# Scan products in four quadrants and a hand-laid engine order in the attention loop of a hybrid attention and delta-net layer

## Chip, cores and metric

One NeuronCore of one Trainium2 chip. The metric is the device time of one execution in microseconds; the measured time is the median of several executions. TensorE has a granted clock with two levels, 1.2 and 2.4 GHz; the profile gives it as a share of the higher one.

## The reference, cut to what matters

One layer over 2048 latent tokens on a grid 64 wide, with 256 context tokens as a prefix, in fp32. Two branches read one input projection: neighbourhood attention (8 heads of 64, a window of 8 x 16 keys plus all context keys in one softmax) and a gated DeltaNet that runs a recurrence over chunks of 64 tokens, forward and backward.

```python
def step(S, xs):                                   # one chunk of the delta rule
    qk_i, qd_i, kd_i, u_i, w_i, gt_i = xs
    v_new = u_i - einsum('bhck,bhkv->bhcv', w_i, S)
    o_i = einsum('bhck,bhkv->bhcv', qd_i, S) + einsum('bhij,bhjv->bhiv', qk_i, v_new)
    S = S * gt_i[..., None, None] + einsum('bhck,bhcv->bhkv', kd_i, v_new)
    return S, o_i
...
s = concat([s_win, s_ctx]); pr = softmax(s)        # attention, per head and query row
o = einsum(p_win, v_band) + einsum(p_ctx, vc)
...
o_dn = _rmsnorm(o_f + rev(o_b)) ; y = sigmoid(g_na)*u_na + sigmoid(g_dn)*u_dn ; x + gate * (y @ w_out)
```

## The kernel before

The program runs in stages: projections of the normed tokens (TensorE), triangular solves on VectorE beside them, neighbourhood keys and bias tables, then a loop over 32 attention units with the recurrence inside it, then the output projections. The change lies in the loop.

An attention unit is 128 queries (8 rows of 16 columns) of four heads, taken as two pairs `pr`. For a pair, `scores` multiplies queries and banded keys as three products of high and low parts into two PSUM tiles `pw`, and VectorE adds the bias table (`tedge` at the grid's rim, `tmid` elsewhere) and takes the maximum (L1078). `scores_ctx` does the same with the context keys (maxima L1085, merged in L1087) and ScalarE takes the four exponentials (L1090, L1093). `turn` transposes the banded weights (L1101, copies L1103), `turn_ctx` those of the context (L1110, copy L1112), `values` multiplies both with the values (L1121, L1125). `sums_inv` inverts the sums and GpSimd spreads them into `rb`; `finish` transposes `rb` and multiplies the output with it and with the gate path (L1141, L1142). The banded keys come in four widths: 288, 360, 384 and 512.

The recurrence is a Python generator, `scan`, of which `pump(chain, n)` runs n pieces between the steps of a unit, so that one step of the recurrence, forward and backward chunk side by side on the two halves of the partitions, falls into each unit. Each piece of products is 16 products of 64x64x64, 8 heads by 2 directions, which the profile shows as 32 matmuls: both state products (L871), the third `p2` (L887, copied to `cw` by ScalarE, L889), `p4` for the state (L894, added in L895) and `p3` for the output (L901, L903). A direction d multiplies on row half d and column half d of the array. GpSimd multiplies the state by its decay (L883) and, in the last 16 units, adds the output of the opposite direction (L881). There `dn_out` also normalises the output of the step before: square (L917), row sums (L919, L920), a power on GpSimd (L922), scaling (L923), transposes (L927), product with the gate path (L928) and a store.

What sets the order: within the loop TensorE runs in the order of the program text (`tc.manual_schedule`). VectorE, ScalarE, GpSimd and SyncE, which issues every DMA, run in the order that the planner lays from its costs and priorities; only the splits of new queries and keys into a high part (ScalarE, L966) and a low part (GpSimd, L967), the weight splits (L1197, L1200) and the gate products (L1165) are kept in program order among themselves. Queries are loaded for two units at a time in even units and split in the odd unit that follows; new key rows are split in units 1 to 5, 9, 10, 13, 14 and 17 to 19. PSUM has 3 tiles `pw`, 2 `pt`, 2 `pc` and 1 `po`; `cr` and `cw` have one buffer, the loaded operands of a step two.

## Time and profile before

| | |
|---|---|
| median of 3 runs | 2399.5 us (2392.4 to 2406.4) |
| the profiled execution | 2395.0 us |
| its span, first to last instruction | 2393.3 us |
| mean granted clock of TensorE | 0.971 |
| busy: TensorE, VectorE, ScalarE, GpSimd | 2197.7, 1501.5, 850.4, 938.6 us |
| the unit loop | about 1478 to 2016 us of the span |

Times below are microseconds from the first instruction of the profiled execution. PE is TensorE's matmuls and PEld its weight loads, DVE is VectorE, ACT ScalarE, POOL GpSimd, SP SyncE. A matmul's end is modelled by the profiler, its start is measured, so distances are taken from start to start. A bracket behind an instruction is the time that its engine stood idle before it and what released it.

### The profile page before, as it was taken

How to read it: one execution, taken by the hardware profiler on the slowest of the kernel's cores; microseconds unless marked ns; L12 is line 12 of the kernel's file. 1: busy time of each engine (PE TensorE's matmuls, PEld its weight loads, DVE VectorE, ACT ScalarE, POOL GpSimd, SP SyncE). 2: the span in 40 equal slices, each digit the busy share in tenths (PEclk: the TensorE clock that was granted, in tenths of full speed). 3: DMA queues.
4: the chain of work that ended last, by engine and by line, in shares of the span. 5: the costliest groups of instructions: out<-in, count | busy, mean ns of one | idle time of the engine just before them, and what ended most of it. 6: DMA issues, size and time to landing. Idle time of an engine off the chain costs nothing. (4 is left out here: it accounts for less than half of the span.)

```text
span 2393.3 us, 47334 instructions
## 1 busy us (share of the span) xinstructions
PE 2197.7 (92%) x18359; PEld 1842.7 (77%) x18359; DVE 1501.5 (63%) x2410; ACT 850.4 (36%) x2624; POOL 938.6 (39%) x784
## 2 busy tenths in 40 slices
PE   6999999998989999999889987899888887999999
PEld 2778777876767778999878866777767776889988
DVE  3736777469959969859759803666566766222222
ACT  4524344344333332434554112444444444211110
POOL 2514777654423102315757410211123335543442
PEclk8999999999999999999999998999999999999999
DMA  7323444665574152154676567777886776444342
GB/s 266 102 75 77 114 123 125 159 154 140 145 189 123 54 128 89 58 133 133 179 185 185 166 166 216 218 195 198 215 209 188 188 199 189 142 118 129 108 115 90
DMA packets 461593, 358.17 MB, mean 150 GB/s; under 512 B 203254, under 2 KB 386698, under 8 KB 460810
## 3 DMA queue, kind: packets, MB, share of 16 engines
q1 hardware_dynamic: 461368, 355.16, 55.3%
q8 instruction: 144, 2.36, 0.4%
q14 instruction: 81, 0.66, 0.1%
HBM read 231.71 MB, written 119.67 MB: 147 GB/s over the span
## 5 line engine op out<-in xcount | busy, mean ns | idle before, releaser
L179 PE MATMUL pd<-hT,slots 128*128 128x512 f32 (+1 forms) x3360 | 813.5, 397 | 1.8 <-ACT hT L319 1.7
L179 PEld LDWEIGHTS pd<-hT,slots 128*128 128x128 f32 x3360 | 619.9, 191 | 147.2 <-issue 3.8
L580 DVE TENSOR_TENSOR tmp<-Xs 128x236 f32<-128x236 f32 (+43 forms) x310 | 315.5, 1018 | 38.7 <-DMA Xs<-d_X 25.9
L582 DVE TENSOR_TENSOR Xs<-Xs,tmp 128x236 f32<-128x236 f32 (+43 forms) x310 | 321.1, 1036 | 8.6
L125 POOL TENSOR_TENSOR slots<-w_raw,slots 128x512 fp32r<-128x512 f32 (+1 forms) x76 | 115.7, 1523 | 348.6 <-ACT slots L124 339.4
L729 PE MATMUL pd<-slots,hT 128*128 128x256 f32 x1248 | 164.0, 292 | 0.0
L729 PE MATMUL pd<-wide,hT 128*128 128x256 f32 x1248 | 159.5, 290 | 2.4 <-ACT wide L124 1.3
L729 PEld LDWEIGHTS pd<-slots,hT 128*128 128x128 f32 x1248 | 158.9, 196 | 0.0
L729 PEld LDWEIGHTS pd<-wide,hT 128*128 128x128 f32 x1248 | 156.4, 196 | 3.2 <-ACT wide L124 1.7
L1090 ACT ACTIVATE pr<-pr,nm 128x288 f32<-128x288 f32 (+3 forms) x128 | 77.9, 609 | 161.4 <-DVE nm L1087 161.4
L883 POOL TENSOR_TENSOR sd<-sd,gts 128x512 f32<-128x512 f32 x36 | 37.6, 1045 | 215.9 <-PE pc L871 198.3
L1346 DVE SCALAR_TENSOR_TENSOR gt<-gt,pu 128x256 f32<-128x256 f32 x120 | 46.3, 418 | 121.0 <-DMA gt<-d_g 73.6
L782 POOL TENSOR_TENSOR tmk<-trr,tmk 128x288 f32<-128x288 f32 (+3 forms) x72 | 98.0, 1378 | 40.1 <-DMA tmk<-in_k_mk_dram 35.5
L484 DVE SCALAR_TENSOR_TENSOR y<-raw,vT,y 128x512 f32<-128x512 f32 (+1 forms) x112 | 95.5, 864 | 24.8 <-ACT raw L472 21.2
L1345 PE MATMUL pu<-ckq,OS 128*128 128x256 f32 x512 | 95.2, 284 | 2.2 <-DVE gt L1346 1.3
L1360 DVE SCALAR_TENSOR_TENSOR ckd<-pf,gate 128x512 f32<-128x512 f32 x32 | 22.0, 692 | 119.7 <-PE pf L1356 111.8
L694 POOL TENSOR_TENSOR nrn<-nss,nhalf 128x8 f32<-128x8 f32 x34 | 72.6, 2135 | 54.7 <-DVE nss L693 54.4
L1347 POOL TENSOR_TENSOR gt<-gt 128x256 f32<-128x256 f32 x60 | 44.3, 738 | 122.3 <-DVE gt L1346 110.3
L205 ACT ACTIVATE zt<-pd 128x512 f32<-128x512 f32 x68 | 40.4, 594 | 142.8 <-PE pd L179 68.8
L1348 ACT CAST yh<-gt 128x256 fp32r<-128x256 f32 x60 | 24.3, 405 | 187.6 <-POOL gt L1347 187.2
L873 DVE TENSOR_TENSOR cr<-pc,egs 128x512 f32<-128x512 f32 x68 | 46.8, 688 | 66.2 <-DMA cT<-d_T 36.0
L1101 PE MATMUL pt<-ident,pr 128*128 128x128 f32 (+2 forms) x416 | 66.3, 286 | 23.5 <-ACT pr L1090 22.4
(295 smaller groups left out, 4612.7 us busy)
## 6 DMA issues: line engine op xcount, KB each, us to landing
w_raw<-in_w_in_dram SPq DMA_DIRECT2D x92, 256.0 KB
ckq<-d_kq SPq DMA_DIRECT2D x64, 256.0 KB
gt<-d_g SPq DMA_DIRECT2D x60, 256.0 KB
d_X<-X SPq DMA_DIRECT2D x72, 128.0 KB
Xs<-d_X SPq DMA_DIRECT2D x18, 512.0 KB
d_g<-zt SPq DMA_DIRECT2D x36, 256.0 KB
cv<-d_v SPq DMA_DIRECT2D x72, 128.0 KB
cT<-d_T SPq DMA_DIRECT2D x72, 128.0 KB
```

The source lines that it names most:

```text
L125: G.tensor_tensor(out=lo[:, j:j + 4, 0:n], in0=wr, in1=hi[:, j:j + 4, 0:n].bitcast(F32), op=ALU.subtract)
L179: PE.matmul(ps[0:n, 0:m], a[:, k, 0:n], h_part(g, z, k), start=k == 0 and i == 0, stop=k == KB - 1 and i == 2)
L484: V.scalar_tensor_tensor(out=y[:, 0:m], in0=raw[:, o + j - 1:o + j - 1 + m], scalar=tap(j), in1=y[:, 0:m], op0=ALU.mult, op1=ALU.add)
L580: V.tensor_tensor(out=tv, in0=X[r, piv, cols].unsqueeze(1).to_broadcast([8 * n, m, w]), in1=X[r, rows, piv].unsqueeze(2).to_broadcast([8 * ...
L582: V.tensor_tensor(out=X[r, rows, cols], in0=X[r, rows, cols], in1=tv, op=ALU.add)
L694: G.tensor_tensor(out=rn, in0=ss, in1=nhalf, op=ALU.pow)
L729: PE.matmul(ps[:, 256 * i:256 * i + 256], h[:, 256 * j + P * i:256 * j + P * i + P], w[:, :, part, k, :], start=k == 0 and n == 0, stop=k ...
L782: G.tensor_tensor(out=mv, in0=rr[:, k0:k0 + nr, w0:w0 + n], in1=mv, op=ALU.add)
L873: V.tensor_tensor(out=t, in0=ps, in1=eg, op=ALU.mult)
L1090: S.activation(e[:, 0:nk], e[:, 0:nk], AF.Exp, bias=nm[:, u:u + 1], accum_out=self.sums[:, hh, 0:1])
L1101: PE.transpose(ptw[0:kb, b, :], self.et[u][:, kb * b:kb * b + kb], ident)
L1345: PE.matmul(ps, a, r[:, k, :], start=k == 0 and n == 0, stop=k == 3 and n == 2)
```

## The change

Four things are changed.

- In a main step of the recurrence the two state products are issued as one group, head by head, the second one with its output on the opposite column half (`half[d ^ z]`), into a second PSUM tile; `p4` and `p3` likewise become one group, `p3` on the opposite half. The output of the two directions therefore lies with its halves swapped, and `dn_tokens` swaps the two halves of its addresses; `egw` holds the growth factors with the halves swapped. The steps over the context tokens keep their groups.
- In the unit, `scores` of the second pair stands between `turn` and `turn_ctx` of the first, `scores` of the next unit between `turn` and `turn_ctx` of the second pair, `values(1)` behind the next unit's `scores_ctx`, and `sums_inv` behind the second `turn`. There are five pumps in a unit instead of seven: the state products ahead of the first turn; `cr` of the second product and the square of `dn_out` behind `scores(1)`; decay, `p2`, `cw`, and row sums, power and scaling of `dn_out` behind `scores_ctx(1)`; the transposes of `dn_out` behind `values(0)`; `p4` and `p3` behind the next `scores(0)`.
- VectorE, ScalarE and GpSimd run in the order of the program text through the loop, as TensorE does. SyncE stays with the planner.
- `turn_ctx` always copies on ScalarE (before: VectorE for the first pair); `rb` has one buffer instead of two; `tedge` is allocated in the pool `ap`, which opens once the projections' pools are closed, instead of `aq`, which opens earlier.

```diff
@@ -187,8 +187,8 @@
         v = d.rearrange("q (n s t) -> q n s t", s=2, t=C)
         c0, n = t0 // C, m // C
         if c0 >= 16:
-            return v[:, c0 - 16:c0 - 16 + n, 0]
-        return v[:, 16 - c0 - n:16 - c0, 1][:, ::-1]
+            return v[:, c0 - 16:c0 - 16 + n, 1]
+        return v[:, 16 - c0 - n:16 - c0, 0][:, ::-1]
 
 
     def gate_col(kind, i, p):
@@ -861,22 +861,24 @@
             main = i >= CCH
             ld = scan_in.pop(i)
             scan_load(i + 1)
-            eg = egs[:, i].unsqueeze(2).to_broadcast([P, H, C])
             half = [slice(C * d, C * d + C) for d in range(2)]
 
-            def times_state(z):
-                ps = pc.tile([P, H, C], F32, name="pc")
-                for h in range(H):
+
+            pss = [pc.tile([P, H, C], F32, name="pc") for _ in range(2 if main else 1)]
+            for h in range(H):
+                for z, ps in enumerate(pss):
                     for d in range(2):
-                        PE.matmul(ps[half[d], h, :], ld["ckq"][half[d], ho(h), z, :], sd[half[d], h, :], start=True, stop=True)
+                        PE.matmul(ps[half[d ^ z], h, :], ld["ckq"][half[d], ho(h), z, :], sd[half[d], h, :], start=True, stop=True)
+
+            def grown(z, e):
                 t = q2.tile([P, H, C], F32, name="cr")
-                V.tensor_tensor(out=t, in0=ps, in1=eg, op=ALU.mult)
+                V.tensor_tensor(out=t, in0=pss[z], in1=e.unsqueeze(2).to_broadcast([P, H, C]), op=ALU.mult)
                 return t
             r = ld["cv"]
-            V.tensor_tensor(out=r, in0=r, in1=times_state(0), op=ALU.subtract)
+            V.tensor_tensor(out=r, in0=r, in1=grown(0, egs[:, i]), op=ALU.subtract)
             yield
             if main:
-                tq = times_state(1)
+                tq = grown(1, egw[:, i - CCH])
                 if i - CCH >= 16:
                     G.tensor_tensor(out=tq.rearrange("p h e -> p (h e)"), in0=tq.rearrange("p h e -> p (h e)"), in1=os_[:, NCH - 1 - i], op=ALU.add)
                 yield
@@ -888,17 +890,18 @@
             w = q2.tile([P, H, C], F32, name="cw")
             S.copy(w, p2)
             yield
+
             p4 = pc.tile([P, H, C], F32, name="pc")
+            p3 = pc.tile([P, H, C], F32, name="pc") if main else None
             for h in range(H):
                 for d in range(2):
                     PE.matmul(p4[half[d], h, :], ld["ckd"][half[d], h, :], w[half[d], h, :], start=True, stop=True)
+                for d in range(2 if main else 0):
+                    PE.matmul(p3[half[1 - d], h, :], ld["cA"][half[d], ho(h), :], w[half[d], h, :], start=True, stop=True)
             V.tensor_tensor(out=sd, in0=sd, in1=p4, op=ALU.add)
-            yield
+            if not main:
+                yield
             if main:
-                p3 = pc.tile([P, H, C], F32, name="pc")
-                for h in range(H):
-                    for d in range(2):
-                        PE.matmul(p3[half[d], h, :], ld["cA"][half[d], ho(h), :], w[half[d], h, :], start=True, stop=True)
                 o = q2.tile([P, H, C], F32, name="co", bufs=2)
                 V.tensor_tensor(out=o, in0=tq, in1=p3, op=ALU.subtract)
                 if i - CCH < 16:
@@ -915,6 +918,7 @@
         def dn_out(t, oa, zd):
             ob = q2.tile([P, H, C], F32, name="ob", bufs=2)
             S.activation(ob, oa, AF.Square)
+            yield
             so = q2.tile([P, H], F32, name="so", bufs=2)
             V.reduce_sum(out=so, in_=ob, axis=AX.X)
             V.tensor_scalar(out=so, in0=so, scalar1=4.0 / 64, scalar2=4.0 * EPS, op0=ALU.mult, op1=ALU.add)
@@ -936,20 +940,22 @@
                 dn = dn_out(*wait.pop()) if wait else iter(())
                 step = scan_step(n) if n < NCH else iter(())
                 next(step, None)
-                next(dn, None)
                 yield
                 for _ in range(2):
                     next(step, None)
+                    next(dn, None)
                     yield
                 next(dn, None)
                 yield
-                yield from step
-                yield
+                next(step, None)
                 yield
 
         egs = qp.tile([P, NCH, H], F32, name="egs")
         gts = qp.tile([P, NCH, H], F32, name="gts")
+        egw = qp.tile([P, NCH - CCH, H], F32, name="egw")
         SP.dma_start(out=egs, in_=d_eg)
+        for d in range(2):
+            SP.dma_start(out=egw[C * d:C * d + C], in_=d_eg[C - C * d:P - C * d, CCH:])
         SP.dma_start(out=gts, in_=d_gt)
         scan_load(0)
         chain = scan()
@@ -1031,7 +1037,7 @@
             elif edge[0] == (hg, rg, o):
                 tab = edge[1]
             else:
-                tab = [aq.tile([P, 2, 384], F32, name=f"tedge{z}") for z in range(2)]
+                tab = [ap.tile([P, 2, 384], F32, name=f"tedge{z}") for z in range(2)]
                 for z in range(2):
                     SP.dma_start(out=tab[z][:, :, 0:nr * w], in_=d_tab[:, ty, 4 * hg + 2 * z:4 * hg + 2 * z + 2, o:o + nr * w])
                 edge[:] = (hg, rg, o), tab
@@ -1103,13 +1109,13 @@
                     (S.copy if u else V.tensor_copy)(pT[0:kb, 0:nb], ptw[0:kb, 0:nb])
                     self.pts.append(pT)
 
-            def turn_ctx(self, pr):
+            def turn_ctx(self):
                 ptx = ptp.tile([P, 2, 2, P], F32, name="pt")
                 for u in range(2):
                     for b in range(2):
                         PE.transpose(ptx[:, u, b, :], self.et[u][:, 512 + P * b:640 + P * b], ident)
                 self.ptc = ap.tile([P, 2, 2, P], F32, name="pTc")
-                (S.copy if pr else V.tensor_copy)(self.ptc, ptx)
+                S.copy(self.ptc, ptx)
 
             def values(self, pr):
                 if pr == 0:
@@ -1129,7 +1135,7 @@
                 V.tensor_tensor(out=ri, in0=self.sums[:, :, 0], in1=self.sums[:, :, 1], op=ALU.add)
                 V.tensor_scalar(out=ri, in0=ri, scalar1=2.0, scalar2=None, op0=ALU.mult)
                 V.reciprocal(ri, ri)
-                self.rb = ap.tile([P, 4, 64], F32, name="rb", bufs=2)
+                self.rb = ap.tile([P, 4, 64], F32, name="rb")
                 G.tensor_copy(self.rb, ri.unsqueeze(2).to_broadcast([P, 4, 64]))
 
             def finish(self):
@@ -1231,6 +1237,8 @@
         un.scores(0)
         un.scores_ctx(0)
         todo, splits = [], []
+        order_all = tc.manual_schedule(engines={mybir.EngineType.DVE, mybir.EngineType.Activation, mybir.EngineType.Pool})
+        order_all.__enter__()
         for n in range(32):
             ahead_splits = []
             hg = n // 16
@@ -1253,37 +1261,37 @@
                 todo[0] = wo_load(todo[0])
             pump(chain, 1)
             un.turn()
-            pump(chain, 1)
-            un.turn_ctx(0)
             un.scores(1)
             pump(chain, 1)
+            un.turn_ctx()
             un.scores_ctx(1)
-            un.sums_inv()
+            pump(chain, 1)
             un.values(0)
-            pump(chain, 2)
+            pump(chain, 1)
             for f in splits:
                 f()
             splits = ahead_splits
             if split_now:
                 wo_split(*split_now)
             un.turn()
+            un.sums_inv()
             nu = Unit(n + 1, *ahead) if ahead else None
-            pump(chain, 1)
-            un.turn_ctx(1)
             if nu:
                 nu.scores(0)
             else:
                 pump(gprod, 1000)
-            un.values(1)
+            pump(chain, 1)
+            un.turn_ctx()
             if nu:
                 nu.scores_ctx(0)
+            un.values(1)
             un.finish()
-            pump(chain, 1)
             un = nu
             pump(gprod, int(n < 17))
 
             if hg:
                 todo += {3: (0,), 7: (1, 2), 11: (3, 4), 15: (5, 6, 7)}.get(n % 16, ())
+        order_all.__exit__(None, None, None)
         order_pe.__exit__(None, None, None)
         for i in (1, 0):
             split(*oz_parts(order[0], i), zraw[:, i])
```

## Rows read from the trace of the kernel before

**Rows 1.** Windows: busy us (instructions) per engine, clock, DMA share, GB/s; the loop.

```profile
1478.00:2016.00 538.00, 478.50 (x7988) 382.75 (x7988) 362.71 (x943) 236.16 (x691) 142.05 (x140) 0.97 0.75 200
```

**Rows 2.** Waits in the loop: who for whom, us in total, times, longest.

```profile
PE pt L1101 <- ACT pr L1090: 22.4, 29, 1.7
PEld pw L1068 <- POOL ql L967: 16.0, 12, 2.4
```

**Rows 3.** Line L1142, to 1740 us and whole: durations, first and last start.

```profile
L1142 DVE TENSOR_TENSOR azt<-po,azt x16: 424/425/426, 1491.1 to 1736.6; 128x256 f32<-128x256 f32 x16
L1142 DVE TENSOR_TENSOR azt<-po,azt x32: 414/425/426, 1491.1 to 2016.8; 128x256 f32<-128x256 f32 x32
```

**Rows 4.** Timeline, TensorE, one unit: start, us, instruction, operands, count.

```profile
1608.39 1.15 PE L871 MATMUL pc<-sd,ckq 64*64 64x64 f32 x32
1609.47 0.66 PE L1110 MATMUL pt<-ident,pr 128*128 128x128 f32 x4
1610.06 0.43 PE L1068 MATMUL pw<-KH,qh 64*128 64x360 f32 x2
1610.74 1.15 PE L887 MATMUL pc<-cv,cT 64*64 64x64 f32 x32
1611.82 0.39 PE L1068 MATMUL pw<-KHc,qh 64*128 64x256 f32 x2
1612.37 0.88 PE L1121 MATMUL po<-pT,vt 120*64 120x128 f32 x12
1613.61 1.15 PE L894 MATMUL pc<-cw,ckd 64*64 64x64 f32 x32
1614.69 0.87 PE L1101 MATMUL pt<-ident,pr 128*120 128x128 f32 x6
1615.49 1.15 PE L901 MATMUL pc<-cw,cA 64*64 64x64 f32 x32
```

**Rows 5.** Timeline, TensorE, a chunk product on all four quadrants.

```profile
485.30 0.98 PE L628 MATMUL kk<-kq 64*64 64x64 f32 x32
```

**Rows 6.** Lines in the loop: instruction, count, busy us, mean ns, idle before.

```profile
L1085 DVE TENSOR_REDUCE mx<-pw 128x1 f32<-128x256 f32 x126 | 47.6, 419 | 34.0 <-PE pw L1068 33.7
L873 DVE TENSOR_TENSOR cr<-pc,egs 128x512 f32<-128x512 f32 x63 | 43.4, 688 | 14.9 <-PE pc L871 14.4
L1078 DVE CUSTOM_DVE_ANT_0 pr<-pw,tmid 128x360 f32<-128x360 f32 (+1 forms) x64 | 36.7, 609 | 18.0 <-PE pw L1068 17.3
L1078 DVE CUSTOM_DVE_ANT_0 pr<-pw,tedge 128x384 f32<-128x384 f32 (+1 forms) x62 | 29.1, 505 | 23.0 <-DMA tedge<-d_tab 11.8 <-PE pw L1068 9.5 <-PE po L1121 1.7
L1090 ACT ACTIVATE pr<-pr,nm 128x384 f32<-128x384 f32 (+3 forms) x126 | 76.9, 611 | 157.0 <-DVE nm L1087 157.0
L1093 ACT ACTIVATE pr<-pw,nm 128x256 f32<-128x256 f32 x126 | 57.1, 456 | 0.0
L889 ACT COPY cw<-pc 128x512 f32<-128x512 f32 x32 | 18.8, 587 | 90.8 <-PE pc L887 90.8
L883 POOL TENSOR_TENSOR sd<-sd,gts 128x512 f32<-128x512 f32 x32 | 33.4, 1045 | 183.5 <-PE pc L871 181.0 <-DMA ckd<-d_kd 2.5
L922 POOL TENSOR_TENSOR ro<-so,nh 128x8 f32<-128x8 f32 x16 | 26.4, 1648 | 34.8 <-DVE so L920 34.4
L881 POOL TENSOR_TENSOR cr<-cr,OS 128x512 f32<-128x512 f32 x16 | 21.3, 1330 | 6.2 <-DMA OS<-co 6.1
L967 POOL TENSOR_TENSOR ql<-fwr,qh 128x512 fp32r<-128x512 f32 x15 | 19.0, 1269 | 0.0
```

**Rows 7.** Timeline and windows, TensorE, two waits and what followed.

```profile
1692.55 0.58 PE L1068 MATMUL pw<-KHc,qh 64*128 64x256 f32 x1 [2.31 <-DVE mx L1078]
1692.50:1696.00 3.50, 3.45 (x29) 2.90 (x31) 1.38 (x5) 1.63 (x6) 0.00 (x0) 0.51 0.77 216
1765.42 0.38 PE L1068 MATMUL pw<-KHc,qh 64*128 64x256 f32 x1 [2.35 <-DVE mx L1078]
1765.40:1768.80 3.40, 3.38 (x61) 2.90 (x61) 1.36 (x5) 1.85 (x7) 0.00 (x0) 1.00 0.53 133
```

## The prediction

> **What bounds the kernel now.** I read in this order: busy time by stage, waits of one engine for another in the unit loop, the distance between units, the timeline of TensorE through one unit, then single operations. Nearly all that the change touches lies in the loop over 32 attention units, from 1478 to 2016 us: there TensorE is busy 478.5 of 538.0 us, VectorE 362.7, ScalarE 236.2, GpSimd 142.1, at a DMA share of 0.75 [rows 1]. So TensorE looks like the bound, but its 60 us of gaps have owners: the weight turn waits 22.4 us for the exponentials, the banded scores 16.0 us for `ql`, the low part of new queries, from GpSimd [rows 2]. The last operation of each unit (L1142) gives the period: (1736.6 - 1491.1) / 15 = 16.37 us over the first 16 units, (2016.8 - 1736.6) / 16 = 17.51 us over the last 16 [rows 3], which have the delta-net output norm on top. Through one unit TensorE goes back to back; from start to start a 32-instruction scan group takes 1.08 us (1608.39 to 1609.47, 1613.61 to 1614.69), the context turn 0.59, scores 0.68, context scores 0.55, values 1.24, a turn 0.80 [rows 4]. Five scan groups, two of each of the others and 0.4 for the transposes of `rb` (an estimate) make 13.5 us; with some 0.9 of wait at the turn a unit takes about 14.4 us where nothing is late, and 0.6 more, an estimate too, in the second half. What gates a unit is TensorE's order and that wait.
>
> **The scan products.** The two state products of a step, and its last two, become two groups of 64 instructions on all four quadrants instead of four groups of 32 on two. Does the array run four at once? In the scan groups it runs two at once: 32 instructions take 1.15 us, the last start included [rows 4]. The nearest row with all four quadrants is the chunk product at 485.30, whose two halves use different column halves: 32 instructions of the same 64x64x64 form take 0.98 us [rows 5], shorter only because the second half starts while the first still runs. So I take 1.15 us for 64 (full overlap), with 2.16 (none) as the other end; below 1.15 a reason excludes it, since each quadrant has as many products as now. Saved: 2 x (1.08 - 0.07) = 2.0 us of TensorE's order in each of 32 units, 65 us in all; 0 at the other end.
>
> The Trainium skill (TensorE: Matmul & The Clock Gate, section "Wait — 56ns, not 53.3ns?") says that starts of matmuls never come closer than about 25 ns, however small they are. By that an estimate for 64 is 1.6 us and the saving 1.1 us a unit; no stretch here sustains more starts than the row at 485.30, which is about at that rate, so the trace doesn't refute it. It has a rival of its own below.
>
> **The order of the other engines.** VectorE, ScalarE and GpSimd now run in the order of the program text. I lay out one unit by the rows, with t = 0 where its first turn starts, right after the 64-instruction group. VectorE: product 0.69, difference as long, copy of the turn 0.6 (near the 0.59 of `cw`), two banded maxima of 0.5 (0.61 for the two widest forms' mean), product 0.69, so it reaches the context maxima, 0.42 each, at 3.7, and their merge ends at 4.6 [rows 6]. ScalarE: four exponentials, 2 x 0.61 + 2 x 0.46 = 2.1, to 6.7, and only then the copy `cw`, 0.59, to 7.3 [rows 6]. TensorE meanwhile, by [rows 4]: turn, scores, context turn to 2.1, context scores (held up 0.4 by a PSUM buffer that the first banded maximum frees) to 3.1, third product to 4.1, values to 5.4; the second turn follows the exponentials to 6.4, the next scores to 7.2, then the double group waits for `cw`: 7.3 to 8.5. VectorE adds state and output, 2 x 0.69, to 10.0, next maxima to 11.0, the two output products and the gate step to 12.8. TensorE is round at 12.4, so VectorE closes the loop: **12.8 us**, 13.0 for the mean of the four key widths. The exposed wait of the turn is gone, since values and the double group now lie between context scores and turn.
>
> **Odd units** split new queries. The copy of `qh` (the size of `cw`, 0.6) now stands behind `cw` on ScalarE, and `ql` (1.27 on GpSimd) behind that: 7.3 + 0.6 + 1.27 = 9.2 [rows 6]. The next scores, which stood far down TensorE's order, now stand right behind the turn and could start at 6.4; everything after them, the double group included, waits: 9.6 instead of 7.2, **15.3 us**. New key rows, in six splits of five odd units of the first half, put another 1.27 on GpSimd ahead of `ql`.
>
> **The second half** has the output norm. Its row sums, power and scaling used to be handed out ahead of the first turn, two scan groups and more before their transposes. Now the row sum (0.7, taken as long as a product over the same 512 columns) stands behind the maxima on VectorE (4.6 to 5.4), and the power on GpSimd behind the addition of the mirrored output (1.33, from 3.7, when the second product is there) and the state's decay (1.05): 3.7 + 1.33 + 1.05 = 6.1, power 1.65 to 7.7, scaling 0.69 to 8.5 [rows 6]. TensorE reaches the transposes of this at 5.4 and **waits 3.1 us**; queued behind them are the second turn, scores, double group, values and the next unit's group, 7.2 us. Period 8.5 + 7.2 = **15.7 us**, 16.1 for the mean width. `ql` is hidden in this wait.
>
> That wait also costs clock. After a wait of 2.31 us at 1692.55 the granted clock was 0.51 for 3.5 us, the 1.2 GHz level, so some 1.7 us of work were lost; after one of 2.35 us at 1765.42 it stayed at 1.00 [rows 7]. For 3.1 us I take three falls in four, at 1.4 us as part of the slow stretch can fall into the wait: 1.05 us a unit (between 0, no fall, and 3.4, two).
>
> **Small edits.** The context copy always on ScalarE takes 0.6 us from VectorE, which stands in the layout. One buffer of `rb` instead of two: written after the next turn, read before; nothing waits. `egw` adds two small loads. `tedge` now lies in the pool that opens after the projections end, so its first loads come later and may hold up the first unit: +2 us, between 0 and 6 (two loads of 288 KB at 200 GB/s [rows 1] are 2.9 us, and as much may be queued ahead). The swapped halves of the d_z and d_oz addresses cost nothing.
>
> **The sum**, against the profiled execution (2395.0 us; span 2393.3). First half: 8 x 13.0 + 8 x 15.3 + 6 x 1.27 = 234 us, plus 0.7 a unit for what comes late by DMA and clock now too (half of 16.4 less a clean 14.9 at the mean width) = 245, against 16 x 16.37 = 262: -17. Second half: 16 x (16.1 + 1.05 + 0.3, an estimate for the weight splits) = 279, against 280: -1. Lead +2. Net -16: 2379; the median of the three runs stands 4.5 above the profiled execution, so **2384**.
>
> **Rivals.**
> The power wait costs no clock, or row sums and power come earlier than laid out: the second half at 16.4, another 17 us less, **2367**. For it: the wait of 2.35 us without a fall [rows 7]. Chance 0.18; the forecast (2367 to 2400) has 0.47.
>
> Slower: the power wait makes the clock fall in each second-half unit, and twice, because the slowed stretch pushes the next unit's first products late against ScalarE. Price 2 x 1.5 = 3.0 us a unit: 16 x (16.1 + 3.0 + 0.3) = 310, +30 instead of -1: **2415**. It decides from where the second half's mean clock lies under about 0.85. For it: a wait longer than any in rows 7. Chance 0.22.
>
> The quadrants don't overlap as four: 64 instructions take up to 2.16 us, 1.0 more for each of two groups. The one at `cw` lies wholly on the loop, the other with 0.4 of cover: 1.6 x 32 = 51 us, **2435**; halfway, 2410. The floor that the Trainium skill states (above) would be a case of it: 0.45 x 2 x 32 = 29 us. Rows 5 speak against. Chance 0.07.
>
> The orders come out much as the planner had them, and only TensorE changes: 2.0 + 0.5 us a unit, 80 us, **2320** with the 4.5; DMA would allow 0.75 x 538 = 403 us [rows 1]. Chance 0.06.
>
> **How the numbers follow.** About 0.5% (12 us) is what can be told from no change, so faster means under 2387.5, slower over 2411.5. Faster: 0.29 of the forecast, 0.18 and 0.06: 0.53. Same: the forecast's rest, 0.18, part of the slow-clock and quadrant cases, 0.09: 0.27. Slower: 0.20. The range 2340 to 2418 leaves out most of the last two rivals and the tail of the slow one.
>
> **What will show it.** Two 64-instruction groups a unit near 1.2 us; L1101 no longer waiting for exponentials at the first turn; in odd units L1068 waiting 2 us for `ql`; in the second half L927 waiting about 3 us for L923 and that for L922, with PEclk under 1 there; periods near 13 and 15 to 17 by turns, then about 17. A second half clearly under 16 us, or groups of over 1.6 us, would prove me wrong.

## The result, and the profile after

The changed kernel takes 2418.9 us (2416.4 to 2423.4 over four runs), the kernel before, beside it on the same chip, 2398.1 (2392.4 to 2406.4): a ratio of 1.009, 95% interval 1.0075 to 1.0105. It is 0.9% slower, where 0.7% faster was forecast. Its profiled execution takes 2419.5 us (span 2417.7), 24.5 more than that of before, and 40 more than the 2379 that the sum gave for it.

All of it lies in the unit loop. The windows of the changed kernel, answering [rows 1], and the last operation of each unit, L1148 now, answering [rows 3]:

```profile
1478.00:2041.00 563.00, 439.36 (x7952) 348.99 (x7952) 368.24 (x908) 253.90 (x721) 143.63 (x139) 0.88 0.73 190
```
```profile
L1148 DVE TENSOR_TENSOR azt<-po,azt x16: 423/424/425, 1486.7 to 1732.2; 128x256 f32<-128x256 f32 x16
L1148 DVE TENSOR_TENSOR azt<-po,azt x32: 423/424/425, 1486.7 to 2040.7; 128x256 f32<-128x256 f32 x32
```

TensorE is busy 439 us instead of 478, and the loop is longer all the same; the granted clock is 0.88 instead of 0.97. The first 16 units keep their (1732.2 - 1486.7) / 15 = 16.37 us, to the hundredth what they took before; the last 16 go from 17.51 to (2040.7 - 1732.2) / 16 = 19.28. The lead, up to the end of the first unit, is 4.4 us shorter. The waits of TensorE, then of VectorE, in the loop (who for whom, us in total, times, longest), beside [rows 2]:

```profile
PE pc L931 <- DVE co L927: 49.2, 15, 5.1
PE pw L1074 <- DVE mx L1084: 42.8, 14, 10.9
PE pt L1116 <- DVE pT L1109: 9.9, 14, 1.1
PE pw L1074 <- POOL ql L973: 9.5, 8, 2.0
PE pw L1074 <- ACT qh L972: 7.9, 5, 2.3
```
```profile
DVE pr L1084 <- DMA tedge<-d_tab: 40.9, 8, 11.3
DVE co L927 <- POOL ro L926: 29.4, 15, 3.9
```

The turn's 22.4 us for the exponentials are gone, as forecast. Two waits took their place: the norm's transposes for the scaling (L931), forecast at about this size, and VectorE's banded maxima for the edge bias tables (11.8 us before, in the last row of the L1078 pair of [rows 6]), for which TensorE then waits at L1074. The latter was not in the forecast. Its largest case, unit 13: SyncE's issues (start, duration) and VectorE's first maximum.

```profile
1676.33 0.36 SPq L1033 DMA_DIRECT2D azt<-d_z  x1
1676.78 1.31 SPq L845 DMA_DIRECT2D ckq<-d_kq  x2
1678.14 0.58 SPq L1042 DMA_DIRECT2D tedge<-d_tab  x1
```
```profile
1686.39 0.56 DVE L1084 CUSTOM_DVE_ANT_0 pr<-pw,tedge 128x384 f32<-128x384 f32 x1 [11.30 <-DMA tedge<-d_tab]
```

The same load in the kernel before:

```profile
1679.29 0.69 SPq L1036 DMA_DIRECT2D tedge<-d_tab  x1
```
```profile
1691.93 0.56 DVE L1078 CUSTOM_DVE_ANT_0 pr<-pw,tedge 128x384 f32<-128x384 f32 x1 [3.02 <-DMA tedge<-d_tab]
```

In both the table comes 8 to 13 us after its issue, and the issue is at nearly the same time. But the changed kernel wants it at 1686.4 - 11.3 = 1675.1, the kernel before at 1688.9: a unit gets there sooner, and within the unit the maxima have moved forward, right behind the first turn. VectorE, in a fixed order, does nothing else meanwhile. There is one place for each pair's table, but that place did not hold the load back: the second pair's maxima of unit 12 had left it at 1663.4, 14.8 us before the issue.

```profile
1662.93 0.45 DVE L1084 CUSTOM_DVE_ANT_0 pr<-pw,tedge 128x288 f32<-128x288 f32 x1
```

In the kernel before the same place came free at 1675.3 and the issue followed 4 us later. So the place was free 12 us sooner and the issue went out only 1.2 us sooner: in between SyncE was issuing other transfers, and it had stood from 1672.8 to 1676.3 at `azt`, whose data is wanted some units later. For the next three waits by length (10.4, 7.8 and 5.6 us) the places were free 16, 13 and 7 us before the issues.

### The profile page after: what moved, and what is told of

Its sections match the earlier page's. It is cut to its first block, busy times and chain, and to the rows that moved or that the text cites. A ratio compares the mean times of both kernels' runs of the same rounds, so it can differ in the third digit from the quotient of the medians.

```text
span 2417.7 us, 47383 instructions
## 1 busy us (share of the span) xinstructions
PE 2157.7 (89%) x18359; PEld 1807.2 (75%) x18359; DVE 1509.2 (62%) x2378; ACT 870.0 (36%) x2656; POOL 940.5 (39%) x784
## 5 line engine op out<-in xcount | busy, mean ns | idle before, releaser
L580 DVE TENSOR_TENSOR tmp<-Xs 128x236 f32<-128x236 f32 (+43 forms) x310 | 316.9, 1022 | 38.7 <-DMA Xs<-d_X 30.2
L883 POOL TENSOR_TENSOR cr<-cr,OS 128x512 f32<-128x512 f32 x16 | 20.4, 1273 | 167.7 <-DVE cr L875 145.0
L124 ACT CAST slots<-w_raw 128x512 fp32r<-128x512 f32 (+1 forms) x76 | 46.6, 613 | 106.9 <-DMA w_raw<-in_w_in_dram 87.1
```

The costliest lines, as they stand in the source:

```text
L580: V.tensor_tensor(out=tv, in0=X[r, piv, cols].unsqueeze(1).to_broadcast([8 * n, m, w]), in1=X[r, rows, piv].unsqueeze(2).to_broadcast([8 * ...
```

## The experiments

Each time stands with its ratio to the kernel before, run beside it, and the ratio's 95% interval. Beside all of them the kernel before took 2398.1 to 2400.6 us, so times of different experiments can be compared to some 3 us. A clean unit is one in which no load is late. Line numbers in rows are each kernel's own.

**Tables left out, in both kernels.** After the first unit no edge table is loaded.

```diff
-            elif edge[0] == (hg, rg, o):
+            elif edge[0]:
```

> The changed kernel, its edge bias tables loaded once, for the first unit, and used for every later edge unit (the reload is left out, so these units get a wrong bias; everything else stays). Theory A (the loss is VectorE, in its fixed order, standing for the table of the next edge unit: 40.9 us in 8 waits, 11.8 in the kernel before): these waits are gone, the units at 1689, 1720, 1757 and 1983 us take 16 to 18 us instead of 20 to 28, and the time is 2370 to 2390. Theory B (the loss is the power chain of the output norm in the second half, 49 us at L931, with the clock it costs; the table waits only overlap with it): 2405 to 2420.

> The kernel before with its edge bias tables loaded once, as in the run noedge (the reload is left out, so later edge units get a wrong bias). If table waits are what separates the two kernels, this one gains little, since it stands 11.8 us for tables: 2385 to 2397, and the changed kernel without reloads (2397) is then 0 to 12 us behind it. If the reloads cost both alike (traffic, not waits), it gains as much as the changed kernel did, 22 us: 2374 to 2382.

The changed kernel: 2396.9 us, 0.9981 (0.9967 to 0.9995). The kernel before: 2384.1, 0.9936 (0.9913 to 0.9959). Both times lie between the two cases that were expected. The changed kernel gains 22 us and the kernel before 16, more than its own 11.8 us of waits; the two are 12.8 us apart, where they were 20.8. Theory A accounts for some 6 to 8 of the 20 us between the two, not for all. The units of the changed kernel without reloads:

```profile
L1148 DVE TENSOR_TENSOR azt<-po,azt x16: 424/424/425, 1486.7 to 1716.0; 128x256 f32<-128x256 f32 x16
L1148 DVE TENSOR_TENSOR azt<-po,azt x32: 424/424/425, 1486.7 to 2009.7; 128x256 f32<-128x256 f32 x32
```

(1716.0 - 1486.7) / 15 = 15.3 us in the first half, 18.4 in the second.

**The power earlier; SyncE's order; both.** In the first the norm's steps go out one pump earlier:

```diff
             G.tensor_tensor(out=ro, in0=so, in1=nh, op=ALU.pow)
+            yield
...
                 next(step, None)
+                next(dn, None)
                 yield
-                for _ in range(2):
-                    next(step, None)
-                    next(dn, None)
-                    yield
+                next(dn, None)
+                next(step, None)
+                yield
+                next(step, None)
+                next(dn, None)
+                yield
```

In the second, `behind(...)` stands around the loads of `azt` (L1033) and `zd` (L912), which keeps them at their place among SyncE's issues. The third has both.

> The changed kernel with one edit: the output norm's squares go out with the first pump of a unit, its row sums and power with the second, ahead of the addition of the mirrored output, its scaling with the third, its transposes stay in the fourth. Theory B (power chain): the wait of the transposes at L931, 49 us in the second half, falls under 10 us, PEclk there rises, a second-half unit without another stall goes from 17.7 to 14.5 to 15.5 us, the time is 2370 to 2390. Theory A (table waits): units that wait for tables keep their 20 to 28 us, since the table's place in the queue of DMA issues is not moved, and wait longer the earlier a unit gets there; the gain is 10 us or less, 2405 to 2420.

> The changed kernel, the loads of azt (L1033) and zd (L912) kept at their place in the program text among the DMA issues, instead of issued as early as they were (azt some three units ahead of its use, where SyncE stands 3 to 4.5 us for the store of the buffer, 23.8 us in all; zd 57.8 us in all). Theory A, in the form that SyncE's standing is what makes the tables late: the table issues behind it come 2 to 4 us earlier, the 40.9 us of table waits fall to 25 to 30, the time to 2400 to 2410. If instead one table buffer and the landing time of 8 to 12 us set it: the waits stay within 5 us and the time at 2412 to 2420.

> The changed kernel with the edits of power_early and of sp_order together. In power_early clean second-half units took 14.3 to 15 us, but some took 23 to 32, where SyncE stood 5 to 6.5 us in each unit for a store of zd and the next loads came late. Theory C (two limits in series, the power chain at 17.7 us a unit and SyncE's issues with its standing at about 17): only both edits together pay, the second half falls from 19.3 to 15.5 to 16.5 us a unit, 45 to 60 us in all, the time is 2360 to 2380, and the table wait of the unit at 1672 us stays. Theory A (tables alone): 2405 to 2415, the sum of the two single edits.

The power alone: 2421.3, 1.0067 (1.0044 to 1.0090), nothing gained. SyncE's order alone: 2411.3, 1.0037 (1.0025 to 1.0049), with 30.2 us of table waits; the waits are as its theory A had them, the time lies between its two cases. Both: 2393.9, 0.9970 (0.9957 to 0.9983), 25 us below the changed kernel, where the sum of the two is 5 (by the ratios 29 and 18): two limits in series, as theory C has it, though at half the size that it gave. In power_early the wait at the transposes is down to 13.9 us and clean second-half units take 14.1 to 15.0 us; but others take 23.7 and 32.3. There SyncE stands (two of its issues, and its waits in the loop):

```profile
1854.10 0.36 SPq L934 DMA_DIRECT2D d_oz<-zd  x1
1860.68 0.37 SPq L912 DMA_DIRECT2D zd<-d_z  x1
```
```profile
SPq L912 <- DMA d_oz<-zd: 59.9, 14, 5.2
```

A store goes out at 1854.1, the next issue is a load of `zd` that waits for stores of `zd`, at 1860.7, and everything behind it comes later by as much. The kernel before has such waits too, 32.6 us at its loads of `zd`. With the loads in program order these waits are gone. The table waits are not (VectorE in sp_order, then in sp_power):

```profile
1683.30 0.56 DVE L1084 CUSTOM_DVE_ANT_0 pr<-pw,tedge 128x384 f32<-128x384 f32 x1 [9.29 <-DMA tedge<-d_tab]
```
```profile
DVE pr L1088 <- DMA tedge<-d_tab: 45.5, 8, 12.4
```

**A second place for narrow tables; splits earlier.** all_three adds to sp_power a place for the second pair's narrow tables in two idle buffers; all_four then moves the splits of queries and key rows up, right behind the first turn.

> The edits of sp_order and power_early, and a second place for the second pair's narrow edge tables (in two idle buffers of 2 KB, the gate's loads using the other two), so that wide and narrow tables no longer wait for each other. By theories A and C together: the table waits fall from 40.9 to under 15 us, the first half from 16.4 to 15.4 us a unit, the second to 15 to 16: 2345 to 2370. If DMA's landing time sets it whatever the buffers: within 8 us of the run with the two edits alone.

> As all_three, and the splits of queries and key rows handed out right behind the first turn instead of behind the second pump but one: ScalarE copies the high part ahead of the exponentials of the second pair, GpSimd subtracts ahead of the output norm's power and the state's decay. In the changed kernel L1074 waits 7.9 us for qh and 9.5 for ql: if that price is a unit's period, odd units lose 1.5 to 2 us, 10 to 20 us below all_three; if the loads of the raw queries land too late for it, ScalarE and GpSimd stand for them and the run is 5 to 20 us above all_three.

2398.0, 0.9984 (0.9970 to 0.9999), and 2394.0, 0.9976 (0.9966 to 0.9987): no gain over sp_power, although all_four's clean units take 12.1 to 13.4 us in the first half. As one wait is taken away, others for loads come up. In all_four, TensorE and VectorE:

```profile
PE po L1139 <- DMA vt<-d_nv: 29.2, 12, 6.8
```
```profile
DVE zd L933 <- DMA zd<-d_z: 19.9, 5, 6.4
DVE pr L1096 <- DMA tedge<-d_tab: 15.6, 4, 5.9
```

(A second run of all_four took 2394.5.)

**Are loads late because too much moves?** All kernels with all their loads had so far taken 16.3 to 17.0 us a unit in the first half, at 200 to 212 GB/s, which looked like a bound by throughput. gate_bytes keeps all issues and takes 3.7 MB away that nothing waits for.

> The changed kernel; of the 16 loads of 256 KB for the gate (L1158), which nothing waits for, the last 14 move only 128x8 values to a place that is not read, and the first two are used again (the gate comes out wrong; the count of issues and all engines' work stay). Theory D (in the first half DMA throughput is the bound: seven kernels so far, clean units of 12.2 to 17 us, all took 16.3 to 17.0 us a unit there at 200 to 211 GB/s, and only the two without table reloads took less): 3.7 MB less at 207 GB/s are 17.7 us, so the first half falls by 0.8 to 1.2 us a unit and the time to 2401 to 2407. Theory A (the place and wait of the edge tables) and theory C (SyncE's issues): within 5 us of 2419.

2420.4, 1.0090 (1.0063 to 1.0116): no gain, and theory D falls in the form in which throughput bounds the half. (Shared out by the cut of the next but one experiment, 33 us for 24 MB, 3.7 MB would be 5 us, about what this run can just tell.)

**Fewer loads, in both kernels.** `cT`, `cA` and `ckd` are loaded for the loop's first step and used for all.

```diff
+                if held:
+                    continue
                 SP.dma_start(out=ld["cT"][kr], in_=d_T[pos(d, ch) // 4, :, pos(d, ch) % 4])
```

> The kernel before, with three of the scan's loads (cT, cA, ckd, 768 KB of some 3.3 MB a unit, and their six issues) made for the first step of the loop only and used for all (the scan comes out wrong; engines do the same work). If the kernel before is held by its engines, as I read its profile, little is gained beyond its waits for data: a unit falls from 16.4 and 17.5 us to the clean 14.2 to 15.5 and 16.5, 2365 to 2380. If DMA holds it throughout: 3.7 us a unit, 2280 to 2300.

> The changed kernel with the same three loads made once. Theory D: without DMA's bound the first half comes down to the clean units, 12.5 and 16.2 to 18.4 us by turns, 15 us in the mean or a little under; the second keeps its 17.7 us of the power chain: 2370 to 2385, so 0 to 15 us from the kernel before with the same cut. If it is still over 2395, DMA's bytes are not what holds it.

2385.4, 0.9942 (0.9923 to 0.9961), and 2385.6, 0.9944 (0.9921 to 0.9966). **Level.** The kernel before gains 14 us, less than expected (its units come down to 16.1 and 17.4 us only): it is mostly held by its engines, not by its loads. The changed kernel gains 33, and its table waits fall to 8.9 us. So the 20 us by which the change is slower go with these loads: its units meet late data that those of before did not. The last operations of the units, of before_light and then of after_light:

```profile
L1146 DVE TENSOR_TENSOR azt<-po,azt x16: 423/424/425, 1490.4 to 1731.7; 128x256 f32<-128x256 f32 x16
L1146 DVE TENSOR_TENSOR azt<-po,azt x32: 411/424/425, 1490.4 to 2009.5; 128x256 f32<-128x256 f32 x32
```
```profile
L1152 DVE TENSOR_TENSOR azt<-po,azt x16: 423/424/425, 1490.5 to 1718.7; 128x256 f32<-128x256 f32 x16
L1152 DVE TENSOR_TENSOR azt<-po,azt x32: 423/424/425, 1490.5 to 2007.8; 128x256 f32<-128x256 f32 x32
```

The change makes the first half 16.09 - 15.21 = 0.88 us a unit faster and the second 18.07 - 17.36 = 0.71 slower.

**Work in TensorE's wait.** 12 products of no use stand ahead of the norm's transposes, in the second half of after_light.

```diff
             un.values(0)
+            for _ in range(12 if n > 16 else 0):
+                PE.matmul(un.po[:, 2, :], ident, ident, start=True, stop=True)
             pump(chain, 1)
```

> The kernel of after_light with 12 products of the 128x128 identity with itself, written to a part of po that is overwritten later, ahead of the output norm's transposes in each second-half unit: TensorE works through most of its 3 to 4 us wait for the norm's scaling instead of standing. If the clock is what the wait costs beside itself (my 1.05 us a unit, more by my slow rival): the second half's granted clock rises from 0.88 to 0.95 or more, its units fall from 18.1 to 16.6 to 17.2 us, the time from 2386 to 2362 to 2373. If the clock costs next to nothing there: 18 us and 2382 to 2392, or more where the extra products outlast the wait.

2366.2, 0.9871 (0.9847 to 0.9895): 19 us faster than after_light, with more work. What a wait does to the clock is seen in one unit of the changed kernel, and in one of warm_light where TensorE worked 2.9 us instead (timeline of TensorE, then the window from the transposes on, its last three numbers the granted clock, the DMA share and GB/s):

```profile
1855.26 1.12 PE L931 MATMUL pc<-ident,co 128*128 128x128 f32 x4 [2.96 <-DVE co L927]
1856.17 1.91 PE L1107 MATMUL pt<-ident,pr 128*128 128x128 f32 x8
1855.20:1858.10 2.90, 2.84 (x14) 2.51 (x14) 1.56 (x5) 0.00 (x0) 0.00 (x0) 0.50 0.55 155
```
```profile
1854.21 2.94 PE L1275 MATMUL po<-ident 128*128 128x128 f32 x24
1857.30 0.66 PE L935 MATMUL pc<-ident,co 128*128 128x128 f32 x4
1857.20:1858.60 1.40, 1.30 (x12) 1.14 (x12) 0.65 (x2) 0.00 (x0) 0.00 (x0) 1.00 1.09 228
```

After the wait the transposes and the turn run at 0.50, the 1.2 GHz level, and take 2.8 us to the start of the next group at 1858.0. At 1.00 they need 1.5: 0.5 for the transposes in the second fence, 1.0 for a turn of eight (at 1864.4 in warm_light). Such falls are the rule: of the 15 waits for the scaling in after_light's second half, 12 show a granted clock of 0.5 to 0.8 over the 2.5 us behind them and 3 show 1.00; in warm_light 14 of the same 15 places show 1.00. The windows of the second half, after_light and warm_light, in the last three columns:

```profile
1740.00:2010.00 270.00, 213.57 (x3729) 171.61 (x3728) 191.92 (x450) 124.77 (x344) 95.34 (x87) 0.88 0.50 133
```
```profile
1740.00:2010.00 270.00, 246.24 (x4139) 204.78 (x4140) 193.51 (x455) 130.82 (x355) 107.92 (x102) 0.97 0.57 149
```

Units go from 18.07 to (1984.8 - 1716.8) / 16 = 16.75 us.

**The products on four quadrants alone**, with the pumps of before and the planner laying the order of the other engines: with all loads, and with the three left out. Both keep the changed kernel's pool for `tedge` and its single buffer of `rb`; what these two small edits do was not tried alone.

> The kernel before with only the products changed: the 64-instruction groups on four quadrants, with the pumps and the planner's order of VectorE, ScalarE and GpSimd as before. If TensorE's order gates the units of the kernel before, as I read its profile, each unit loses up to 2.0 us: 2335 to 2360. If the chain from the state through VectorE and ScalarE gates it, the groups go faster (1.16 us for 64) and TensorE waits more: 2380 to 2398.

> The kernel of before_light (2385) with the products on four quadrants alone, pumps and the planner's orders of the other engines as before. If TensorE's order gates a unit, as I took it from the profile of before: 2 us a unit where loads are not late, 2320 to 2345. If the turn's wait for the exponentials and the copies closes the loop on the other engines: the saved 2 us turn into longer TensorE waits and a lower clock, 2370 to 2395, and quads_alone's 2418 was then 20 us of late loads on top.

2417.8, 1.0063 (1.0047 to 1.0078), and 2382.3, 0.9927 (0.9906 to 0.9948). With all loads the products alone are as slow as the whole change (2418.9), which neither of the two cases had. The late loads come with them: VectorE waits for tables

```profile
DVE pr L1085 <- DMA tedge<-d_tab: 27.0, 7, 7.8
```

against 11.8 us before, and SyncE stands 56.5 us for stores of `zd`, against 32.6. Where loads are not late, 2 us less in TensorE's order of each unit are worth 3 us in the whole loop, no more than these runs can tell from nothing. TensorE waits for the other engines instead (quads_light, then before_light):

```profile
PE pt L1112 <- ACT pr L1101: 20.6, 30, 1.7
PE pc L904 <- DVE zd L935: 20.0, 15, 2.6
PE pt L1121 <- ACT pT L1114: 19.4, 22, 1.9
PE pt L1121 <- DVE pT L1114: 18.6, 28, 2.5
```
```profile
PE pt L1105 <- ACT pr L1094: 21.0, 29, 1.7
PE pw L1072 <- POOL ql L971: 12.0, 11, 2.0
PE pt L1114 <- DVE pT L1107: 10.8, 14, 1.4
PE pc L905 <- DVE zd L932: 4.8, 6, 1.0
```

The turn's wait for the exponentials is as long as it was. What grew are the waits ahead of the context turn for the copies of the turn, and that of the last product group for `zd`: a group of 64 takes both PSUM tiles `pc` at once, and the output norm's product must have left one.

**Who makes the loads late?** tables_act lets ScalarE issue the edge tables, right behind the maxima that free their place; all_four_light has all_four's edits and the three loads left out; all_four_few puts six issues of 64x8 values a unit back in their place.

> The changed kernel, the edge tables of the next unit issued by ScalarE right behind the second pair's banded maxima of this one, which free their place, instead of by SyncE, where they stand behind some 10 us of issues a unit and behind loads that wait for stores. Theory E (SyncE's in-order queue makes the tables late): from issue to use there is then a whole unit, 12 to 16 us, against 8 to 12 us of landing; the 40.9 us of table waits fall under 15, the time to 2385 to 2402. If the landing time is set by what is in the DMA queues whoever issues: tables land later than 12 us after the issue, the waits stay over 25, the time is 2405 to 2420.

> The kernel of all_four (2394) with cT, cA and ckd loaded once: the run that all_light was meant to be (under that label the kernel of all_four was run a second time by mistake). If late loads hold all_four: both halves come down to its clean units, 12.2 to 13.4 us and 14.1 to 15.8, 2300 to 2325, 60 us or more under the kernel before with the same cut (2385). If its engines or the clock hold it: 2340 or more.

> The kernel of all_four_light with six small issues a unit put back in the place of those taken out (cT, ckd and cA of both directions, 64x8 values each to a place that is not read), so that SyncE issues as often as in all_four while 768 KB less move. Theory E (SyncE's issues and their order make loads late): back to near all_four's 2394, 2375 to 2395. If the bytes moving through the DMA engines make them late: it stays near 2323, at most 2340.

tables_act: 2439.9, 1.0182 (1.0154 to 1.0211). VectorE's waits for tables are down to 5.4 us, but ScalarE stood at its own issues, and what it does next came late:

```profile
1684.43 1.11 ACTq L1038 DMA_DIRECT2D tedge<-d_tab  x2
1685.63 0.58 ACT L1123 COPY pTc<-pt 128x512 f32<-128x512 f32 x1 [9.22 <-DMA tmid<-d_tab]
```

So this run doesn't tell whose queue matters. The other two do: all_four_light 2322.7, 0.9690 (0.9667 to 0.9714); all_four_few 2361.6, 0.9849 (0.9824 to 0.9874). From all_four's 2394, taking 768 KB a unit of bytes away gives 32 us, and taking the six issues of SyncE away on top of it another 39. Neither theory holds alone: by this pair, bytes and issues make all_four's loads late in about equal parts. The two are not wholly apart. At the small issues (L855) SyncE stood 70 us in all, by the profile until earlier transfers had landed, as in all_four it stands 38 us at those of `cT` and 22 at those of `ckd`. Its two longest entries:

```profile
SPq L855 <- DMA vt<-d_nv: 25.9, 22, 2.3
SPq L855 <- DMA ckq<-d_kq: 13.4, 27, 1.0
```

The small issues are also kept in program order among other loads, as those they replace were not; what part of the 39 us that is, no run shows. Without late loads, the change with its repairs is some 62 us under the kernel before with the same cut. Its units:

```profile
L1164 DVE TENSOR_TENSOR azt<-po,azt x16: 424/424/425, 1488.5 to 1687.8; 128x256 f32<-128x256 f32 x16
L1164 DVE TENSOR_TENSOR azt<-po,azt x32: 411/424/425, 1488.5 to 1940.9; 128x256 f32<-128x256 f32 x32
```

13.3 us in the first half and 15.8 in the second, against 16.1 and 17.4 of before_light.

**What can be had with all loads.** sp_power's edits, the early splits, and 6 products in TensorE's wait.

> The changed kernel with the loads of azt and zd in program order, the power early, the splits early, and 6 products of the identity with itself (1.5 us) ahead of the output norm's transposes in the second half; the edge tables as in the change. sp_power (2394) had PEclk 0.93 in the second half and 22 us of waits of those transposes for the scaling. If the clock matters there as in warm_light (20 us), it gains 5 to 12 us and the early splits 4: 2378 to 2388, 0.5% to 0.9% under the kernel before. If late loads hold each unit anyway: 2390 to 2398.

2387.2, 0.9959 (0.9941 to 0.9977): 0.4% under the kernel before, 32 us under the change as it was made, and the fastest of those with all loads. The table waits are still there (48.1 us in 10 waits).

## Why the prediction was wrong

By its own steps:

- **The scan products: right in the size, wrong in the worth.** 64 instructions on four quadrants take what the row at 485.30 promised [rows 5]:

```profile
1610.19 1.16 PE L871 MATMUL pc<-sd,ckq 64*64 64x64 f32 x64
```

  1.09 us to the start of the next group, 17 ns from start to start. The floor of about 25 ns that the Trainium skill states (TensorE: Matmul & The Clock Gate, section "Wait — 56ns, not 53.3ns?") would have made 1.6 us, an estimate; the trace disagrees, and that rival is out. But the first paragraph's conclusion, "what gates a unit is TensorE's order and that wait", did not hold for the kernel before: the 2.0 us a unit that the edit saves were worth 3 us in all, quads_light against before_light. When TensorE comes sooner, it waits longer, not at the turn but for its copies and for `zd`. (The 16.0 us for `ql` in [rows 2] are the weight loads'; the matmuls waited 12.0.) The forecast itself did not rest on those 65 us, since it laid the new order out and let VectorE close the loop; the rival of 2320 did.
- **Even units: right.** 12.8 us, 13.0 at the mean width, were forecast; of the first six, four take 12.4 to 12.6 and two 13.8 and 14.3.
- **Odd units: the layout right, the clock after their wait left out.** Forecast 15.3, and 16.6 with key rows; without rows they take 16.2, with rows mostly 18.3 to 18.5. Unit 7, without rows, waits 1.17 us for `qh` and 0.76 for `ql` and takes 16.2; in after_light it waits 1.35 and 0.75 and takes 14.7, under the forecast. The clock behind the wait is the difference (last three columns as above; changed kernel, then after_light):

```profile
1592.20:1595.20 3.00, 3.00 (x72) 2.54 (x70) 1.89 (x6) 0.00 (x0) 0.00 (x0) 0.51 0.52 155
```
```profile
1594.80:1597.80 3.00, 3.00 (x84) 2.46 (x86) 2.37 (x7) 0.59 (x1) 0.29 (x1) 1.00 0.02 5
```

  The forecast charged a fall of the clock for the power wait and none for this one, beyond what its 0.7 a unit may hold.
- **"0.7 a unit for what comes late by DMA and clock now too": this is the term that failed.** It took the lateness of before as a constant of the kernel: 11 us in the first half, and nothing in the second. By after_light, late loads cost 16 x (16.37 - 15.21) = 19 us in the first half and 16 x (19.28 - 18.07) = 19 in the second. The lateness is no constant: a load's landing follows its issue, the issue follows SyncE's queue, and a faster unit reaches the data sooner than the queue delivers. The first half was to take 245 us; it took 16 x 16.37 = 262, as before. With the three loads left out it takes 243, without table reloads 245, where the layout without lateness had 234: the other 9 us lie mostly in the odd units with key rows, where after_light still has some late loads.
- **The edge tables: wrong in place.** "Later by +2" was priced for the first unit, which in fact ends 4.4 us earlier. That the step "banded scores ahead of the context turn" also moves the maxima forward against the table's load, while the load keeps its place in SyncE's queue, was not priced. By noedge against before_noedge it is 6 to 8 us of the 20.
- **The power wait: right.** Forecast 3.1 us in each unit of the second half; 49.2 us over 15. Clean units there take some 17.7, forecast 17.45.
- **The clock: somewhat short.** 1.05 us a unit were forecast, three falls in four; in after_light 12 of 15 fell, and filling the wait gives 18.07 - 16.75 = 1.3. The slow rival had two falls in every unit, 3.0, which no run shows. Its 310 us for the second half were met (308), but 19 of them are late loads, so its 2415 is near the measured time mostly for another reason. The second half's granted clock is 0.87, above the 0.85 from which that rival was to decide.
- **The end of the loop** was not forecast: the last unit takes 24.7 us, 18.8 before. In the fixed order the gate's last products stand in the middle of it, and VectorE waits 3.2 us there for `mod_b` (read in after_light). That this is the whole of the 5.9 us was not tried.

In sums, for the profiled execution: forecast 2379, measured 2419.5, 40 us more. The first half is 17 us over its forecast, the second 308 - 279 = 29, the lead 6 under. Of the first half's 17, late loads are 8 (19 less the 11 allowed for) and the odd units 9, with the clock and what lateness is left in after_light. Of the second half's 29, late loads are 19; the other 10 are, by estimate, 4 for the clock and 6 for the last unit. The two mechanisms shown by runs are late loads, 20 us against the kernel before, and the clock after the power wait, 19 to 20 us, of which the forecast had 17. Not settled is by how much SyncE's queue and by how much the traffic sets the landing of a given table; the two shares were measured on all_four alone. Nor was it tried whether the new pool of `tedge` has a part in when its loads are issued.

## What to carry to other kernels

In a tuned loop, price a faster unit against its loads as well as its engines: for each single-buffered load take the time from the issue to the landing, and from the instruction that frees its place to the one that wants it, and see whether the new period still fits. Look at where in its queue the issue goes out, too: here a place was free 15 us before its load was issued. Removing work from the engine that looks busiest may only lengthen its waits; lay out the whole loop before counting such a gain, and look at the clock, because the clock can fall in waits that TensorE did not have before. A repair that gains nothing alone may be half of one that does: here the early power and SyncE's order gave some 5 us one by one and 25 together.

## What the runs showed of the hardware

- Adding 12 products of 128x128 a unit ahead of a wait made a kernel 19 us faster: the granted clock of the second half rose from 0.88 to 0.97.
- 64 matmuls of 64x64x64 on four quadrants take 1.16 us, as long as 32 on two [rows 4].
- In tables_act ScalarE stood at its table issues, in one case from 1676.4 to 1684.4, though the maxima that free the place had ended at 1678.2; the profile names loads that SyncE had issued (`tmid`, `oa`, `fwr`) as what released it. Why it stood, no run here shows.
- Six issues a unit that move next to nothing made a kernel 39 us slower, 2322.7 to 2361.6; SyncE stood 70 us at them, by the profile until earlier transfers had landed.
